# Segment mean over 10 million sorted ids: probe loads in eleven small groups between the data tiles, looks and gathers 18 rows ahead, no ring clear, branch at row 82

## The chip, the cores and the metric

The kernel runs on one core of a Trainium2 chip. The metric is the device time of one execution in microseconds (us), lower is better. "Span" is the profiled execution's own length; the time is 1.7 to 1.8 us longer. Runs were made on several chips. The changed kernel took the same time on two occasions, but the kernel before has slower states, told below, so each comparison says what it compares.

Names: VectorE (DVE), ScalarE (ACT), GpSimd (POOL), SyncE (SP, which here only issues loads).

## The reference

```python
def reference(data, segment_ids):          # 10,000,000 floats; sorted ids below 10,000
    num_segments = int(segment_ids.max()) + 1
    sums = np.zeros(num_segments, dtype=np.float32)
    counts = np.zeros(num_segments, dtype=np.float32)
    np.add.at(sums, segment_ids, data)
    np.add.at(counts, segment_ids, 1)
    return sums / np.maximum(counts, 1)
```

## The kernel before

Each of 128 partitions holds 78125 elements, cut into 98 "rows" of 800. A row has at most one boundary between two segments. To find it without reading all 80 MB of ids, the kernel

1. **probes**: loads every 160th id, 8 bytes at a time (5 columns a row, 489 in all), in row groups;
2. **looks** (`first_look`, VectorE, nine small operations): from a group's probes it finds which block of 160 holds the boundary, and writes an index;
3. **gathers** (GpSimd, one indirect DMA a row): fetches the 159 ids of that block into a ring of 36 row slots;
4. **looks a second time** (`second_look`, VectorE, six rows at once): sums the gathered ids, which gives the boundary `KK`;
5. **splits** (VectorE, one a row): sums the data left of the boundary; ScalarE sums the whole row (`total`).

At the end come carries, counts and two tables that are written out. A general path sits in a branch that is not taken with this input.

```python
GROUPS = [6, 8, 12, 12, 12, 12, 12, 12, 12]
RING = 36
...
    dpool = ctx.enter_context(tc.tile_pool(name="dpool", bufs=18))   # 18 data tiles of 2 rows
...
    GT = gpool.tile([P, RING, W], I64, name="GT")
    nc.gpsimd.memset(GT.bitcast(I32).rearrange("p a b -> p (a b)"), 0)
...
    def load_probes(g):
        a = 0 if g == 0 else K * bounds[g] + 1
        b = min(K * bounds[g + 1] + 1, NPR)
        nc.sync.dma_start(out=pr_flat[:, a:b], in_=ids_p[:, a * S : (b - 1) * S + 1 : S])
...
    def gather(g):
        for r in range(bounds[g], bounds[g + 1]):
            nc.gpsimd.indirect_dma_start(
                out=GT[:, r % RING, :], out_offset=None, in_=ids2d[:],
                in_offset=bass.IndirectOffsetOnAxis(ap=IDX[:, r : r + 1], axis=0),
                bounds_check=N - W, oob_is_err=False)

    def second_look(a, b):
        s = a % RING
        nc.vector.tensor_reduce(
            out=GS[:, a:b], in_=gt32[:, s : s + b - a, 0 : 2 * W : 2], axis=AX.X, op=ALU.add)
        kr = fpool.tile([P, b - a], FP32, name="kr")
        nc.vector.tensor_sub(out=kr, in0=QQ[:, a:b], in1=GS[:, a:b])
        nc.vector.tensor_mul(out=KK[:, a:b], in0=kr, in1=BT[:, a:b])

    def split(r):
        ...
        nc.vector.scalar_tensor_tensor(
            out=junk_v[:, 0:n], in0=iota[:, 0:n], scalar=KK[:, r : r + 1], in1=d,
            op0=ALU.is_lt, op1=ALU.mult, accum_out=A[:, r : r + 1])
...
    for r in range(-6, NR):
        while nt < NT and nt <= (r + 24) // 2:
            load_data(nt)
            nt += 1
            if pnext < NG:                       # one probe group after each early data tile
                load_probes(pnext)
                pnext += 1
        while lnext < NG and bounds[lnext] <= r + 30:
            first_look(lnext)
            lnext += 1
        while gnext < NG and bounds[gnext] <= r + 16:
            gather(gnext)
            gnext += 1
        ...
        if r >= done_k: second_look(done_k, min(done_k + 6, NR)); ...
        total(r); split(r)
        ...                                      # check at row 60, branch at 64, first table at 65
```

The program's order is not the order on an engine: the framework's scheduler emits each engine's instructions by its own estimate of when they will be ready, with program order as priority. Each engine then executes its list in that order.

## Time and profile before

| | before |
|---|---|
| time, fast runs | 231.4 us median (230.1 to 231.7) |
| span; VectorE busy | 230.0; 150.9 us |
| first gather starts, last ends | 19.7, 164.3 us |
| first split; splits left 4 us after the last gather | 62.3 us; 40 |
| last VectorE operation; tail after it | 217.4; 12.6 us |

The page first: 40 slices of 5.75 us, each digit the busy tenths of a slice; the last line is GB/s moved by the DMA.

```profile
span 230.0 us, 1186 instructions
...
DVE  4963102204298960351999999999299999999800
...
POOL 8914777777778777777878788788400000000110
DMA  6899999999999999999999999999749000000000
GB/s 81 102 142 144 231 160 204 239 131 230 237 124 375 409 397 397 398 403 402 399 400 402 399 403 401 401 399 412 303 170 369 14 0 0 0 0 0 2 5 0
```

The VectorE is idle for most of the first 60 us and solid, but for one slice, from about 109 us (slice 19, counted from 0) on. The DMA moves little in the first 70 us, while the 8-byte probes pass, then 400 GB/s.

The groups of the page (line, engine, operation, output<-input, count, then busy us and mean ns of one, then idle time before them and what ended most of it):

```profile
L324 POOL DMA_INDIRECT GT<-in_segment_ids_dram,IDX x98 | 115.0, 1174 | 36.8 <-issue 26.2
...
L295 DVE CAST q_114<-pr 128x13 f32<-128x13 int32 (+2 forms) x8 | 9.0, 1127 | 40.5 <-DMA pr<-in_segment_ids_dram 40.5
L335 DVE TENSOR_REDUCE GS<-GT 128x6 f32<-128x954 int32 (+1 forms) x17 | 18.7, 1099 | 23.1 <-DMA GT<-in_segment_ids_dram,IDX 21.5
...
L281 POOL MEMSET GT<- 128x11448 int32 x1 | 9.6, 9628 | 0.0
```

The clear (L281) takes 9.6 us. While it runs, the first cast of the VectorE does not end (start, length):

```profile
2.79 9.63 POOL L281 MEMSET GT<- 128x11448 int32 x1
```

```profile
4.83 7.62 DVE L295 CAST q_114<-pr 128x7 f32<-128x7 int32 x1 [2.39 <-DMA pr<-in_segment_ids_dram]
```

The waits (who waited for whom: total us, times, longest):

```profile
DVE q_114 L295 <- DMA pr<-in_segment_ids_dram: 40.5, 7, 8.3
...
DVE GS L335 <- DMA GT<-in_segment_ids_dram,IDX: 21.5, 4, 6.3
POOL GT L324 <- DVE IDX L315: 7.3, 1, 7.3
```

The VectorE waits mostly for probes.

The VectorE's timeline near the first split (start, length, ..., idle before it and releaser):

```profile
52.66 0.17 DVE L295 CAST q_114<-pr 128x13 f32<-128x13 int32 x1 [7.89 <-DMA pr<-in_segment_ids_dram]
...
53.76 0.17 DVE L315 SCALAR_TENSOR_TENSOR IDX<-NB,pos 128x12 int32<-128x12 f32 x1
54.06 1.15 DVE L335 TENSOR_REDUCE GS<-GT 128x6 f32<-128x954 int32 x1
61.59 0.17 DVE L295 CAST q_114<-pr 128x13 f32<-128x13 int32 x1 [6.38 <-DMA pr<-in_segment_ids_dram]
...
62.31 1.04 DVE L350 SCALAR_TENSOR_TENSOR junk_v<-iota,q_114,data_t 128x800 bf16<-128x800 f32 x1
```

The look of a later group (L295, index at L315) stands in front of the first second look (L335), and one more stands behind it, before the first split. The engine sits up to 8.3 us for a group's probes although the gathers of row 0 landed long before.

### The profile page before, as it was taken

Reading aid. Unit: us, or ns where it says so; the run is one execution under the profiler, and the core shown is the slowest. Engines: PE = TensorE matmul, PEld = TensorE weight load, DVE = VectorE, ACT = ScalarE, POOL = GpSimd, SP = SyncE. Lnnn points to the kernel's source line nnn. Section 1 sums busy time; section 2 is a strip of 40 time slices with the busy share of each in tenths; the row PEclk is TensorE's granted clock in tenths of the full one; section 3 lists DMA queues with packets and bytes.
Section 4 is the critical chain, followed back from the end, with each engine's and each line's share of the span. In section 5 each row is a group of like instructions: output and inputs, shape, how many; then the busy total and the mean of one; then the engine's idle time right before and its main releaser. Section 6 shows DMA issues by size and latency. Waiting matters only on the chain. (4 is left out here: it accounts for less than half of the span.)

```text
span 230.0 us, 1186 instructions
## 1 busy us (share of the span) xinstructions
PE 1.6 (1%) x6; PEld 1.4 (1%) x6; DVE 150.9 (66%) x432; ACT 95.4 (41%) x197; POOL 128.9 (56%) x114
## 2 busy tenths in 40 slices
PE   0000000000000100000000010000000000000000
PEld 0000000000000100000000000000000000000000
DVE  4963102204298960351999999999299999999800
ACT  2333023033032767676777787667746600000000
POOL 8914777777778777777878788788400000000110
DMA  6899999999999999999999999999749000000000
GB/s 81 102 142 144 231 160 204 239 131 230 237 124 375 409 397 397 398 403 402 399 400 402 399 403 401 401 399 412 303 170 369 14 0 0 0 0 0 2 5 0
DMA packets 74701, 53.39 MB, mean 232 GB/s; under 512 B 65274, under 2 KB 65357, under 8 KB 74688
## 3 DMA queue, kind: packets, MB, share of 16 engines
q1 hardware_dynamic: 69920, 40.51, 62.1%
q0 software_dynamic: 4768, 12.78, 19.2%
q14 instruction: 13, 0.11, 0.2%
HBM read 56.46 MB, written 0.04 MB: 246 GB/s over the span
## 5 line engine op out<-in xcount | busy, mean ns | idle before, releaser
L324 POOL DMA_INDIRECT GT<-in_segment_ids_dram,IDX x98 | 115.0, 1174 | 36.8 <-issue 26.2
L345 ACT ACTIVATE junk_a<-data_t 128x800 bf16<-128x800 f32 x98 | 85.0, 867 | 85.7 <-DMA data_t<-in_data_dram 81.7
L350 DVE SCALAR_TENSOR_TENSOR junk_v<-iota,q_114,data_t 128x800 bf16<-128x800 f32 x98 | 101.8, 1038 | 0.6
L295 DVE CAST q_114<-pr 128x13 f32<-128x13 int32 (+2 forms) x8 | 9.0, 1127 | 40.5 <-DMA pr<-in_segment_ids_dram 40.5
L335 DVE TENSOR_REDUCE GS<-GT 128x6 f32<-128x954 int32 (+1 forms) x17 | 18.7, 1099 | 23.1 <-DMA GT<-in_segment_ids_dram,IDX 21.5
L556 POOL DMA_INDIRECT out_dram<-out_139,AN x1 | 1.1, 1117 | 52.5 <-DVE FF L511 52.5
L345 ACT ACTIVATION_READ_ACCUMULATOR junk_a<-data_t 128x1 f32 x98 | 18.3, 186 | 0.0
L281 POOL MEMSET GT<- 128x11448 int32 x1 | 9.6, 9628 | 0.0
L298 DVE TENSOR_TENSOR eq<-pr 128x48 f32<-128x48 int32 (+2 forms) x9 | 9.2, 1025 | 0.0
L350 DVE DVE_READ_ACCUMULATOR junk_v<-iota,q_114,data_t 128x1 f32 x98 | 7.9, 81 | 0.0
L340 DVE TENSOR_TENSOR q_114<-kr,q_114 128x6 f32<-128x6 f32 (+1 forms) x17 | 2.7, 161 | 0.0
L339 DVE TENSOR_TENSOR kr<-QQ,GS 128x6 f32<-128x6 f32 (+1 forms) x17 | 2.7, 157 | 0.0
L301 DVE TENSOR_SCALAR ST<-jc 128x12 f32<-128x12 f32 (+2 forms) x9 | 2.1, 239 | 0.0
L556 POOL DMA_INDIRECT out_dram<-out_140,AN x1 | 1.0, 992 | 2.0 <-issue 2.0
L310 DVE TENSOR_SCALAR NB<-q_114 128x12 f32<-128x12 f32 (+2 forms) x9 | 1.8, 200 | 0.0
L300 DVE TENSOR_REDUCE jc<-eq 128x12 f32<-128x48 f32 (+2 forms) x9 | 1.7, 194 | 0.0
L345 ACT ACT_TABLE_LOAD x1 | 1.3, 1283 | 0.8 <-PEq L652 0.8
L314 DVE TENSOR_TENSOR pos<-ST,wb 128x12 f32<-128x12 f32 (+2 forms) x9 | 1.5, 164 | 0.1
L309 DVE TENSOR_TENSOR q_114<-q_114 128x12 f32<-128x12 f32 (+2 forms) x9 | 1.5, 166 | 0.1
L318 DVE SCALAR_TENSOR_TENSOR QQ<-q_114,ST 128x12 f32<-128x12 f32 (+2 forms) x9 | 1.5, 164 | 0.1
L315 DVE SCALAR_TENSOR_TENSOR IDX<-NB,pos 128x12 int32<-128x12 f32 (+2 forms) x9 | 1.5, 164 | 0.0
L527 DVE TENSOR_REDUCE out_139<-sel_133 128x48 f32<-128x624 f32 (+1 forms) x2 | 1.3, 628 | 0.0
(95 smaller groups left out, 29.5 us busy)
## 6 DMA issues: line engine op xcount, KB each, us to landing
data_t<-in_data_dram SPq DMA_DIRECT2D x48, 800.0 KB, 11.7
GT<-in_segment_ids_dram,IDX POOLq DMA_INDIRECT x98, 6.1
data_t<-in_data_dram SPq DMA_DIRECT2D x1, 662.5 KB
pr<-in_segment_ids_dram SPq DMA_DIRECT2D x6, 60.0 KB, 11.2
pr<-in_segment_ids_dram SPq DMA_DIRECT2D x1, 58.0 KB, 11.0
pr<-in_segment_ids_dram SPq DMA_DIRECT2D x1, 40.0 KB
pr<-in_segment_ids_dram SPq DMA_DIRECT2D x1, 31.0 KB, 4.0
snt<-in_segment_ids_dram SPq DMA_DIRECT2D x1, 1.0 KB
```

What stands on the lines that cost most here:

```text
L281: nc.gpsimd.memset(GT.bitcast(I32).rearrange("p a b -> p (a b)"), 0)
L295: nc.vector.tensor_copy(out=V[:, a : b + 1], in_=pr32[:, a : b + 1, 0])
L298: nc.vector.tensor_tensor(out=eq, in0=in0b, in1=in1b, op=ALU.is_equal)
L301: nc.vector.tensor_scalar(out=ST[:, a:b], in0=jc, scalar1=float(S), scalar2=float(1 + W), op0=ALU.mult, op1=ALU.add)
L310: nc.vector.tensor_scalar(out=NB[:, a:b], in0=BT[:, a:b], scalar1=-1.0, scalar2=1.0, op0=ALU.mult, op1=ALU.add)
L324: nc.gpsimd.indirect_dma_start(out=GT[:, r % RING, :], out_offset=None, in_=ids2d[:], in_offset=bass.IndirectOffsetOnAxis(ap=IDX[:, r : r ...
L335: nc.vector.tensor_reduce(out=GS[:, a:b], in_=gt32[:, s : s + b - a, 0 : 2 * W : 2], axis=AX.X, op=ALU.add)
L339: nc.vector.tensor_sub(out=kr, in0=QQ[:, a:b], in1=GS[:, a:b])
L340: nc.vector.tensor_mul(out=KK[:, a:b], in0=kr, in1=BT[:, a:b])
L345: nc.scalar.activation(out=junk_a[:, 0:n], in_=d, func=ACT.Copy, accum_out=T[:, r : r + 1])
L350: nc.vector.scalar_tensor_tensor(out=junk_v[:, 0:n], in0=iota[:, 0:n], scalar=KK[:, r : r + 1], in1=d, op0=ALU.is_lt, op1=ALU.mult, accum_ ...
L556: nc.gpsimd.indirect_dma_start(out=out2d[:], out_offset=bass.IndirectOffsetOnAxis(ap=AN[:, i : i + 1], axis=0), in_=o[:], in_offset=None,)
```

## The change

The intent: start splitting early. Probes come in smaller groups between the data tiles, 26 rows ahead, so that only 28 rows' worth stands before row 0 in program order. Looks and gathers come together, 18 rows ahead. The clear goes, as ids that are not gathered are multiplied by zero. The branch moves behind all loads and gathers.

```diff
-GROUPS = [6, 8, 12, 12, 12, 12, 12, 12, 12]
+GROUPS = [4, 6, 8, 10, 10, 10, 10, 10, 10, 10, 10]
+X_PROBE = 26
+X_LOOK = 18
...
-    nc.gpsimd.memset(GT.bitcast(I32).rearrange("p a b -> p (a b)"), 0)
...
-    IF_AT = 64
+    CHECK_AT = 78
+    IF_AT = 82
...
-    for r in range(-6, NR):
-        while nt < NT and nt <= (r + 24) // 2:
+    for r in range(-X_PROBE, NR):
+        while pnext < NG and bounds[pnext] <= r + X_PROBE:
+            load_probes(pnext)
+            pnext += 1
+            if pnext == 2:
+                nc.sync.dma_start(out=snt[0 : P - 1, :], in_=...)
+        while nt < NT and 2 * nt <= r + X_PROBE:
             load_data(nt)
             nt += 1
-            if pnext < NG:
-                load_probes(pnext)
-                pnext += 1
-        while lnext < NG and bounds[lnext] <= r + 30:
+        while lnext < NG and bounds[lnext] <= r + X_LOOK:
             first_look(lnext)
+            gather(lnext)
             lnext += 1
-        while gnext < NG and bounds[gnext] <= r + 16:
-            gather(gnext)
-            gnext += 1
...
-        if r == IF_AT - 4:
+        if r == CHECK_AT:
             keys(); check()
         if r == IF_AT:
-            counts(0, 60)
             with tc.If(...): general_path(...)
-        if r == C1 - 1:
-            counts(60, C1)
+            counts(0, C1)
             ...                                  # first table
```

More of the change, by code (lines that the diff above doesn't have):

```diff
@@ L565 @@
     NT = (NR + 1) // 2
-    load_probes(0)
     nc.vector.memset(snt32[:, 0:1], NSEG)
     nc.vector.memset(snt32[:, 1:2], 0)
-    nc.sync.dma_start(
-        out=snt[0 : P - 1, :],
-        in_=segment_ids[D : N].rearrange("(p d) -> p d", d=D)[:, 0:1],
-    )
-    load_data(0)
-    load_probes(1)
-    load_data(1)
-    load_probes(2)
-    nt = 2
-    IF_AT = 64
+    CHECK_AT = 78
+    IF_AT = 82
     C1 = 66
@@ L584 @@
     lnext = 0
-    pnext = 3
-    for r in range(-6, NR):
-        while nt < NT and nt <= (r + 24) // 2:
+    pnext = 0
+    nt = 0
+    for r in range(-X_PROBE, NR):
[3 more added lines that the diff above has]
+            if pnext == 2:
+                nc.sync.dma_start(
+                    out=snt[0 : P - 1, :],
+                    in_=segment_ids[D : N].rearrange("(p d) -> p d", d=D)[:, 0:1],
+                )
+        while nt < NT and 2 * nt <= r + X_PROBE:
             load_data(nt)
             nt += 1
-            if pnext < NG:
-                load_probes(pnext)
-                pnext += 1
-        while lnext < NG and bounds[lnext] <= r + 30:
+        while lnext < NG and bounds[lnext] <= r + X_LOOK:
             first_look(lnext)
+            gather(lnext)
             lnext += 1
-        while gnext < NG and bounds[gnext] <= r + 16:
-            gather(gnext)
-            gnext += 1
         if r < 0:
@@ L610 @@
             extend()
-        if r == IF_AT - 4:
+        if r == CHECK_AT:
+            assert lnext == NG
             keys()
@@ L614 @@
         if r == IF_AT:
-            counts(0, 60)
+            assert nt == NT
             with tc.If(nc.values_load(badi[0:1, 0:1], min_val=0, max_val=1) > 0):
```

## The prediction

> **What bounds the kernel now.** Span 230.0 us (the page), VectorE (DVE) busy 150.9 of it. The timeline has three stretches. (1) To about 62 us no row is split: the DVE waits 40.5 us for probes (the waits view). Probes are 8-byte reads, 489 columns x 128 = 62592 packets, all queued ahead of the first nine data tiles. In 10:70 us (the stretches view) the DMA moved about 11.0 MB, 27 us at the later 401 GB/s; the other 33 us went to 418 probe columns, 0.078 us a column, about 9.8 ns a packet on each of 16 engines. The Trainium skill (DMA: Bandwidth & Descriptors, Bandwidth) gives a floor of about 10.5 ns a packet; this agrees. (2) 62:102 us: only about 15 rows split; the DVE waits three times 5 to 6 us for gathers that GpSimd issues one per 1.3 us. (3) 102:217 us: DVE nearly solid, 83 rows at about 1.4 us (split 1.10, second look 1.25 per six rows, the rest looks, check, tables), less one 4.0 us hole at the branch. The DMA ends at 178 us, after a dry hole of 5 us: its queue engine lost 12 us at the branch. 12.6 us follow the last DVE operation. So the time is the late DVE start plus DVE work, not DMA.
>
> **What the change does.**
> - The 9.6 us GpSimd clear goes. It blocked the first DVE cast for 7.6 us; the Trainium skill (SBUF — State Buffer, Who interferes with whom) calls this an exclusive lock. With smaller first probe groups, the first gather should start near 6 to 8 us instead of 19.7.
> - Probes keep all their packets (38 us by the estimate), but only groups of rows 0 to 27 stand before row 0 in the DVE's order. First split near 20 to 28 us instead of 62.
> - Two more first looks: 2 to 3 us DVE. Gathers unchanged.
> - The branch at 82 comes after all loads and gathers are issued: no dry hole; a DVE hole of 2 to 4 us may stay.
>
> **New bound.** The DMA: 52.9 MB at 401 GB/s = 132 us, plus 38 us probes, plus 2 us start: about 172 us, 1.75 us a row, more than the DVE's 1.4. So the DVE becomes DMA-paced, with a lag: a look at group b waits for its probes, which land just before data row b, and rows b-18 and on may stand behind it in the DVE's order. The last probes (row 88) should land near 156 us. After that 18 to 28 rows are to be split at 1.3 us, with second looks, and up to 12 us of check, counts and tables: DVE ends near 190 to 206 us. Plus 12.6 us tail and 1.5 us from span to time: 204 to 220; if rows are scheduled closer to their data, 192 to 204.
>
> **Predicted: 206 us, 196 to 217.** Faster by over 2%: 0.90; within 2%: 0.06; slower: 0.04.
>
> **What would show it.** First gather before 9 us, first split before 30; no 7.6 us cast; DMA busy to about 172 us without a hole, at about 300 GB/s throughout; DVE gaps spread out, ended by probes and gathers; last DVE operation near 192; same packets and bytes.
>
> **What would make it wrong.** The instruction order on the DVE is the scheduler's, not the program's: a look placed too early makes the DVE wait in order, once per group, and could return the gain. The probes' time may hide behind other transfers, or grow when mixed. The branch at 82 may drain the pipeline. Buffers (18 tiles) could throttle loads if the DVE lags by over 36 rows.

## More of the kernel before

The 98 gathers keep GpSimd busy 115 us. With the 0.3 us between two of them (the 26.2 us "issue") they form a stream that is hardly ever kept waiting by an index.

GpSimd waits for an index once, at the start.

Counted in the emitted order, seven of the nine groups' indices are written before the first split, the other two after 3 and 23 splits. That makes the start late. It also means that GpSimd always has indices for many rows ahead.

## The result and the profile after

| | before | after |
|---|---|---|
| time, fast runs | 231.4 us (4 runs) | 254.2 us (253.9 to 254.4, 4 runs) |
| ratio | | 1.0995 (95%: 1.096 to 1.103) |
| first gather starts | 19.7 | 13.1 |
| first split | 62.3 | 27.7 |
| gaps of over 0.5 us in the gather stream | none | 9, 65.3 us in sum |
| last gather ends | 164.3 | 216.1 |
| splits left 4 us later | 40 | 13 |
| last VectorE operation | 217.4 | 239.8 |
| tail | 12.6 | 12.6 |

A ratio is the mean time of one kernel's fast runs over that of the other's of the same rounds, so not quite the ratio of the medians. A gap is the idle time on GpSimd between the end of one gather and the start of the next.

The sum closes. The last gather ends 51.8 us later: it starts 6.6 us earlier, has 65.3 us of gaps more, and the gathers with their small pauses take 6.9 us less (-6.6 + 65.3 - 6.9 = 51.8). After it 23.8 us pass until the VectorE is done, instead of 53.1: 29.4 us less. Together 22.4 us, which is the difference of the last VectorE operations.

The page, slices now of 6.3 us:

```profile
span 252.4 us, 1192 instructions
...
DVE  3220843861992495509708834975791991699900
...
POOL 3077157386047518710871574077377387100120
DMA  7999999999999999999999996783223223100000
GB/s 149 233 321 303 385 149 395 286 290 396 184 384 348 215 411 206 352 399 180 413 256 303 352 196 230 246 295 103 62 64 82 62 64 94 46 0 0 0 8 0
```

The VectorE starts early but is solid for no more than two slices on end until it has only 20 us of work left. GpSimd shows a hole every few slices. The DMA's load has fallen to a third or less for the last quarter of the span, so it is not what ends last.

The groups of the changed kernel's page that answer to those of before (L325 is the gather, L336 the second look, L296 the look's first cast):

```profile
L325 POOL DMA_INDIRECT GT<-in_segment_ids_dram,IDX x98 | 110.9, 1132 | 102.3 <-DVE IDX L316 29.0
...
L336 DVE TENSOR_REDUCE GS<-GT 128x6 f32<-128x954 int32 (+1 forms) x17 | 18.8, 1107 | 84.4 <-DMA GT<-in_segment_ids_dram,IDX 83.2
...
L296 DVE CAST q_114<-pr 128x11 f32<-128x11 int32 (+3 forms) x10 | 1.7, 168 | 7.8 <-DMA pr<-in_segment_ids_dram 7.8
```

And its waits, in the columns of before:

```profile
DVE GS L336 <- DMA GT<-in_segment_ids_dram,IDX: 83.2, 14, 11.9
...
POOL GT L325 <- DVE IDX L316: 29.0, 4, 10.5
...
POOL GT L325 <- DVE q_114 L341: 18.8, 2, 11.7
...
DVE q_114 L296 <- DMA pr<-in_segment_ids_dram: 7.8, 2, 6.2
```

The second looks now wait 83.2 us in all for gathers (21.5 before). The gathers' own idle time rose from 36.8 to 102.3 us, for operations of the VectorE: the index, or the operation next to it in the list. The waits for probes nearly vanished, from 40.5 to 7.8 us. So both engines wait, and for each other.

One round of it in the timeline, VectorE first:

```profile
113.52 1.15 DVE L336 TENSOR_REDUCE GS<-GT 128x6 f32<-128x954 int32 x1 [6.54 <-DMA GT<-in_segment_ids_dram,IDX]
114.58 0.16 DVE L296 CAST q_114<-pr 128x11 f32<-128x11 int32 x1
...
119.24 0.17 DVE L316 SCALAR_TENSOR_TENSOR IDX<-NB,pos 128x10 int32<-128x10 f32 x1
...
124.75 0.08 DVE L351 DVE_READ_ACCUMULATOR junk_v<-iota,q_114,data_t 128x1 f32 x1
133.73 1.15 DVE L336 TENSOR_REDUCE GS<-GT 128x6 f32<-128x954 int32 x1 [8.89 <-DMA GT<-in_segment_ids_dram,IDX]
```

and GpSimd over the same stretch:

```profile
106.97 1.00 POOL L325 DMA_INDIRECT GT<-in_segment_ids_dram,IDX  x1 [0.30 <-issue]
119.67 1.64 POOL L325 DMA_INDIRECT GT<-in_segment_ids_dram,IDX  x1 [11.70 <-DVE q_114 L341]
...
132.74 1.00 POOL L325 DMA_INDIRECT GT<-in_segment_ids_dram,IDX  x1 [0.30 <-issue]
```

Read the two together. At 113.52 the second look of rows 42 to 47 starts, after 6.54 us of waiting: those rows' gathers were issued last at 106.97, and GpSimd then had nothing to do. Only behind that wait stands the look for rows 48 to 57 (114.58). Its nine operations are spread between four splits, so its index is written at 119.24. GpSimd resumes at 119.67, after 11.70 us of idleness. It now issues ten gathers. On the VectorE five more splits stand before the next second look; it ends them at 124.8 and then waits 8.89 us for the sixth gather. Then the round begins anew, once per group.

Counted in the emitted order, the number of splits that stand before a group's index:

| first row of the group | 10 | 18 | 28 | 38 | 48 | 58 | 68 | 78 | 88 |
|---|---|---|---|---|---|---|---|---|---|
| after: splits before its index | 5 | 9 | 21 | 30 | 40 | 50 | 61 | 70 | 79 |

So an index is written 5 to 9 rows ahead of the group's first row, not 18. Raising `X_LOOK` from 18 to 26 makes the scheduler emit exactly the same order on VectorE, GpSimd, ScalarE and SyncE, so it was not run (this was seen by building both sources; it is no measurement): 18 is a priority, and it was not what held the looks back.

### The profile page after: what moved, and what is told of

It reads as the page before. It is cut to its first block, busy times and chain, and to the rows that moved or that the text cites. A ratio compares the mean times of both kernels' runs of the same rounds, so it can differ in the third digit from the quotient of the medians.

```text
span 252.4 us, 1192 instructions
## 1 busy us (share of the span) xinstructions
PE 1.6 (1%) x6; PEld 1.4 (1%) x6; DVE 144.3 (57%) x443; ACT 95.4 (38%) x197; POOL 115.2 (46%) x113
## 2 busy tenths in 40 slices
DMA packets 74733, 53.39 MB, mean 212 GB/s; under 512 B 65306, under 2 KB 65389, under 8 KB 74720
## 3 DMA queue, kind: packets, MB, share of 16 engines
q0 software_dynamic: 4768, 12.78, 18.3%
## 5 line engine op out<-in xcount | busy, mean ns | idle before, releaser
L325 POOL DMA_INDIRECT GT<-in_segment_ids_dram,IDX x98 | 110.9, 1132 | 102.3 <-DVE IDX L316 29.0
L336 DVE TENSOR_REDUCE GS<-GT 128x6 f32<-128x954 int32 (+1 forms) x17 | 18.8, 1107 | 84.4 <-DMA GT<-in_segment_ids_dram,IDX 83.2
L296 DVE CAST q_114<-pr 128x11 f32<-128x11 int32 (+3 forms) x10 | 1.7, 168 | 7.8 <-DMA pr<-in_segment_ids_dram 7.8
L299 DVE TENSOR_TENSOR eq<-pr 128x40 f32<-128x40 int32 (+3 forms) x11 | 2.1, 187 | 0.0
L301 DVE TENSOR_REDUCE jc<-eq 128x10 f32<-128x40 f32 (+3 forms) x11 | 2.0, 186 | 0.0
L302 DVE TENSOR_SCALAR ST<-jc 128x10 f32<-128x10 f32 (+3 forms) x11 | 1.8, 168 | 0.0
L310 DVE TENSOR_TENSOR q_114<-q_114 128x10 f32<-128x10 f32 (+3 forms) x11 | 1.8, 167 | 0.0
L319 DVE SCALAR_TENSOR_TENSOR QQ<-q_114,ST 128x10 f32<-128x10 f32 (+3 forms) x11 | 1.8, 162 | 0.0
L311 DVE TENSOR_SCALAR NB<-q_114 128x10 f32<-128x10 f32 (+3 forms) x11 | 1.8, 163 | 0.0
L315 DVE TENSOR_TENSOR pos<-ST,wb 128x10 f32<-128x10 f32 (+3 forms) x11 | 1.8, 162 | 0.0
L316 DVE SCALAR_TENSOR_TENSOR IDX<-NB,pos 128x10 int32<-128x10 f32 (+3 forms) x11 | 1.8, 161 | 0.0
## 6 DMA issues: line engine op xcount, KB each, us to landing
pr<-in_segment_ids_dram SPq DMA_DIRECT2D x7, 50.0 KB, 16.2
```

The lines of the kernel that those rows point to most:

```text
L299: nc.vector.tensor_tensor(out=eq, in0=in0b, in1=in1b, op=ALU.is_equal)
L301: nc.vector.tensor_reduce(out=jc, in_=eq, axis=AX.X, op=ALU.add)
L302: nc.vector.tensor_scalar(out=ST[:, a:b], in0=jc, scalar1=float(S), scalar2=float(1 + W), op0=ALU.mult, op1=ALU.add)
L310: nc.vector.tensor_sub(out=BT[:, a:b], in0=V[:, a + 1 : b + 1], in1=V[:, a:b])
L311: nc.vector.tensor_scalar(out=NB[:, a:b], in0=BT[:, a:b], scalar1=-1.0, scalar2=1.0, op0=ALU.mult, op1=ALU.add)
L325: nc.gpsimd.indirect_dma_start(out=GT[:, r % RING, :], out_offset=None, in_=ids2d[:], in_offset=bass.IndirectOffsetOnAxis(ap=IDX[:, r : r ...
```

## The experiments

**One part at a time.** Theory T1: the looks have too little lead, because their probes stand behind data tiles in the load queue. Rivals: R1, mixing 8-byte packets with the rest slows the transfers; R2, the late branch.

*e1: probes issued 44 rows ahead.*

```diff
-X_PROBE = 26
+X_PROBE = 44
+X_DATA = 26
...
-        while nt < NT and 2 * nt <= r + X_PROBE:
+        while nt < NT and 2 * nt <= r + X_DATA:
```

> The changed kernel with only the probe loads moved: issued 44 rows ahead of use instead of 26 (data tiles stay at 26, looks and gathers at 18). In the emitted VectorE order the looks of the ten-row groups then stand 14 to 22 rows ahead of their first row instead of 7 to 9. Theory T1 (too little lead: the look of a group stands in the VectorE order so close to the group's use that its gathers, 1.3 us each on GpSimd plus about 6 us landing, are waited for once a group): VectorE waits for gathers fall from 83 us to under 30, time about 200 to 212 us. Rival R1 (mixing 8-byte probes and gathers with data slows the transfers themselves): time stays within 2% of the changed kernel, 249 to 259 us. Rival R2 (the late branch and the tables behind it cost the time): stays at 245 to 255.

Measured: 241.2 us, correct. Looks did move (splits before the index of row 38: 17 instead of 30). But the waits of the second looks (L337 here) fell little:

```profile
DVE GS L337 <- DMA GT<-in_segment_ids_dram,IDX: 73.6, 12, 11.8
```

Gaps of the gather stream: 42.7 us. T1's number failed: leading looks alone recover little, because the scheduler now places the second looks earlier as well (rows 36 to 41 after 19 splits). The time lies below both rivals' ranges too, but on another chip than the changed kernel's, so it does not rule them out.

*e2: the clear put back into the changed kernel.*

> The changed kernel with only the GpSimd clear of the gather ring put back. On the chip the clear should cost up to 10 us at the start if only its busy time matters (rival: same or up to 4% slower than the changed kernel). But the emitted VectorE order moves with it: looks stand about 3 to 6 rows earlier (the look of rows 28 on after 15 splits instead of 21). T1 therefore expects it to be FASTER than the changed kernel: 25 to 50 us fewer gather waits, time 220 to 238 us.

Measured: 244.1 us (243.3 to 245.3), correct. Against 254.2 for the changed kernel (on other chips) it is faster, as T1 said and the rival did not, but by less than T1's range. Gaps 58.6 us, waits for gathers 62.9. So removing 9.6 us of work had cost time here. The emitted order moved with the clear (the index of row 28 after 15 splits instead of 21); that the order is how it cost time is argued, as clear and order changed together.

*e3: the kernel before, only the clear taken away.*

> The kernel before with only the clear taken away. Its emitted VectorE order changes too: only 4 groups of looks stand before the first split instead of 7, and the looks from row 38 on stand 25 to 48 rows ahead instead of 38 and more. T1 expects the lead to stay long enough, so the earlier start counts: first split about 40 us instead of 62, and time 205 to 222 us. Rival (the clear is what costs or protects by itself, order does not matter): 222 to 231, that is at most 8 us less than before.

Measured: 216.7 and 218.4 us in fast runs, 226.4 and 226.6 in slow ones, correct. Four looks, not seven, stand before the first split; first split at 36.5 us, no gap in the gather stream, last gather ends at 166.1 us. The longer lead is kept and the early start counts, as T1 expected.

*e4: the kernel before, check, branch and first table moved.*

> The kernel before with only the check at row 78, the branch at 82 and the first table behind it. R2 (the late branch costs): slower by 10 to 20 us. T1: within 2% of before, 227 to 236 us; the tables move behind the branch but the VectorE has the same work and stays busy from 100 us on; the 12 us hole of the load queue at the branch should disappear.

Measured: 250.4 us, correct. Neither theory may claim it. The order changed too: the second looks of rows 66 to 83 moved up to after 24 to 26 splits. Yet its waits for gathers were only 8.8 us in all (21.5 in the trace of before). What its trace shows instead is the stepping state described under e8, from 62 to 112 us: 11 splits start there, 19 in the trace of before. e14 and e15 test the branch properly.

On the chip of these four the kernel before took 239.8 to 241.9 us in the runs labelled fast, 4% more than on the others, where runs at 240 to 242 are labelled slow. The changed kernel was not run on it. The ratios (1.002 for e1, 1.015 for e2, 1.041 for e4) therefore say less than the traces.

**Hold the second looks back.** If second looks in front of looks are the trouble, a pin can test it. One column of an earlier split's result is copied into the second look's output before it, so the scheduler cannot place it earlier than that split:

```diff
     def second_look(a, b):
         s = a % RING
+        if a >= 4:
+            nc.vector.tensor_copy(out=GS[:, a : a + 1], in_=A[:, a - 4 : a - 3])
         nc.vector.tensor_reduce(out=GS[:, a:b], ...)
```

*e5: the changed kernel again.*

> The changed kernel again, unaltered, as the yardstick for the other three on this chip (the second chip ran the kernel before 4% slower than the first). Expected: 1.08 to 1.12 times the kernel before of the same rounds; nine gaps of over 0.5 us in the GpSimd gather stream, about 65 us in sum.

Measured: 254.2 us (252.1 to 254.4), nine gaps, 66.1 us. Only one run of the kernel before was fast in this job (232.6 us; the others 239.7 to 255.8), so 1.09 rests on one run.

*e6: the changed kernel with the pin at 4.*

> The changed kernel with one edit: each second look is pinned behind the split of the row 4 before its first (a one-column copy from that split's result into its output makes it wait), so that the scheduler cannot hoist second looks ahead of splits. Refined theory T1b: the loss is starvation of the GpSimd gather stream: looks stand in the VectorE's order behind second looks that wait for the previous gathers, so both engines wait in turn, and each look stands only 8 to 10 rows ahead of its use. The pin does not move the looks (still 8 to 10 rows ahead), so T1b expects little: gaps of the gather stream 50 to 75 us, time within 4% of the changed kernel (1.05 to 1.14 of before). Rival R4 (the hoisted second looks alone are the loss, the lead of the looks does not matter): 1.00 or below.

Measured: 221.9 us (221.4 to 222.2), correct. Gaps 33.9 us, and the waits view has for the second look

```profile
DVE GS L338 <- DMA GT<-in_segment_ids_dram,IDX: 41.3, 7, 11.2
```

against 83.2 us. My expectation was wrong: the time is 22 us below its range. The indices stand within two splits of where they stood (row 48 after 40 splits in both, row 88 after 78 instead of 79). What moved further are second looks: that of rows 42 to 47 from after 36 splits to after 41, so behind the next group's look. T1b's starvation is right, its stress on the lead is not: the relative order of the two kinds of look decides. R4 had forecast this result (0.95 of the one fast run of before). R1 falls with it, as the transfers are mixed as before.

*e7: e1 and e6 together.*

> Both edits: probes issued 44 rows ahead instead of 26, and second looks pinned. With the first alone (earlier run, 1.00 of before) looks stood 14 to 22 rows ahead, but second looks were hoisted behind them, still 74 us of waits. With both, 13 to 15 splits lie between a look and the second look that needs its gathers. T1b: gaps in the gather stream under 25 us, VectorE waits for gathers under 35 us, 0.88 to 0.94 of before. R4 and R1 (transfers slowed by the mixing): 0.98 or more.

Measured: 214.9 us (214.3 to 215.0), correct: 0.92 of the one fast run of before. Gaps 3.8 us. Its waits view for the look (L297) and the second look (L339):

```profile
DVE q L297 <- DMA pr<-in_segment_ids_dram: 30.1, 8, 6.0
...
DVE GS L339 <- DMA GT<-in_segment_ids_dram,IDX: 13.9, 3, 11.8
```

Waits for gathers are down to 13.9 us, of which 11.8 are the first second look's. The VectorE now waits for probes, that is for the load queue. This comes close to the DMA-paced kernel that the prediction described: the DMA moved 301 GB/s between 160 and 180 us and almost nothing after. R4 and R1 had 0.98 or more here; so the lead counts as well, once the second looks are held back.

*e8: the kernel before without the clear, with the pin at 4.*

> The kernel before without the clear (earlier run: about 0.90 of before, first split at 36 us, gather stream without gaps but 36 us of VectorE waits after the first split), with second looks pinned as well. T1b: same first split within 3 us, gather stream still without gaps, VectorE waits for gathers fall from 37 to under 20 us; 0.84 to 0.89 of before. If the pin does not help: 0.89 to 0.92.

Measured: 217.4 to 217.6 us in four fast runs, 0.935 of the one fast run of before, and no better than e3 (on another chip). Both ranges of the expectation failed. The profile fell in the one slow run (228.5 us span), so its waits are not compared with e3's. What it shows of the slow state, on the VectorE:

```profile
83.16 1.05 DVE L351 SCALAR_TENSOR_TENSOR junk_v<-iota,q,data_t 128x800 bf16<-128x800 f32 x1 [4.38 <-issue]
...
85.95 0.20 DVE L299 TENSOR_REDUCE jc<-eq 128x12 f32<-128x48 f32 x1 [1.66 <-remote]
88.75 1.05 DVE L351 SCALAR_TENSOR_TENSOR junk_v<-iota,q,data_t 128x800 bf16<-128x800 f32 x1 [2.60 <-remote]
```

From about 55 to 105 us the VectorE steps forward by a few operations and then stands, for up to 4.4 us. For the longer of these waits the profile names no operation of another engine of this core that ended them ("issue", "remote"), while GpSimd goes on issuing gathers, 1.3 to 2.0 us apart until 93 us. No fast run of e8 was profiled; in the fast profile of e3, splits of that stretch that wait for no gather follow at about 1.1 us.

**Dose and response.** T1c: what counts is that the look stands before the second look that waits for the previous group's last gathers. A recurrence by hand gives numbers: walk the emitted VectorE order with measured durations (split 1.05 us, second look 1.15); ten gathers follow an index at 1.31 us each; a gather lands about 5 us after its issue ends; transfers of data and probes are left out. It is an estimate from the traces. It was fitted to nothing, but e1, e2 and e5 to e8 had run when it was made; e9 and e10 had not. Recomputed from the order in the traces, every figure below came out within 1.3 us.

*e9: pin at 2.*

> The changed kernel with second looks pinned behind the split 2 rows before their first, instead of 4 (e6: 221.9 us, gaps of the gather stream 33.8 us). Theory T1c, revised after e6: what counts is what stands in the VectorE's order between the look of a group and the second look that waits for the previous group's last gathers; the look must come first. Hand recurrence from measured durations (gathers 1.31 us apart after their look, landing about 5 us after issue, splits 1.05, second look 1.15, VectorE in order, transfers left out), which gives gaps of 71 us for the changed kernel (measured 66) and 33 for e6 (measured 34), gives 15 us of gaps here: 12 to 22 us of gaps, waits for gathers 22 to 35 us, time 208 to 219 us, now near the limit of the transfers. Rival R5 (any pin helps equally, it only evens out the order): within 2% of e6, 217.5 to 226.

Measured: 219.3 us (ratio 0.946), correct. Gaps 29.8 us: outside my range, as was the time by 0.3 us. Waits for gathers 25.1 us, inside. The VectorE now waited 22.6 us for probes, which the recurrence leaves out; an index behind such a wait comes late.

*e10: pin at 6.*

> The same with the pin 6 rows before: the emitted order is nearly the changed kernel's own; looks in the same places within one split, second looks at most 5 splits later. T1c: recurrence gives 54 us of gaps (changed kernel 71, e6 33): 48 to 60 us of gaps, time 233 to 246 us. R5: 217 to 226.

Measured: 233.1 us in three fast runs (ratio 1.007; a slow one took 235.6), correct; gaps 51.9 us: both inside. Waits for gathers were 60.9 us. R5 is out. This is nearly the changed kernel's order, which makes one group a clean pair. The VectorE's timeline of e10 around the index for rows 48 on (L338 is the second look here):

```profile
102.93 0.08 DVE L353 DVE_READ_ACCUMULATOR junk_v<-iota,q,data_t 128x1 f32 x1
102.93 0.17 DVE L296 CAST q<-pr 128x11 f32<-128x11 int32 x1
...
107.58 0.08 DVE L353 DVE_READ_ACCUMULATOR junk_v<-iota,q,data_t 128x1 f32 x1
107.58 0.16 DVE L316 SCALAR_TENSOR_TENSOR IDX<-NB,pos 128x10 int32<-128x10 f32 x1
107.66 1.14 DVE L338 TENSOR_REDUCE GS<-GT 128x6 f32<-128x954 int32 x1
```

and GpSimd's:

```profile
100.53 1.08 POOL L325 DMA_INDIRECT GT<-in_segment_ids_dram,IDX  x1 [0.31 <-issue]
108.01 1.00 POOL L325 DMA_INDIRECT GT<-in_segment_ids_dram,IDX  x1 [6.41 <-DVE IDX L316]
```

The look still starts after 37 splits (36 in the changed kernel) and writes its index after 41 (40). But the second look of rows 42 to 47 (107.66) now stands behind it instead of in front, and the gap on GpSimd is 6.41 us instead of 11.70.

| | emitted order gives (gaps) | measured gaps | time |
|---|---|---|---|
| changed kernel | 71 | 65.3 | 254.2 |
| e2 clear | 68 | 58.7 | 244.1 |
| e10 pin 6 | 54 | 51.9 | 233.1 |
| e1 probes 44 | 42 | 42.7 | 241.2 |
| e6 pin 4 | 33 | 33.9 | 221.9 |
| e9 pin 2 | 15 | 29.8 | 219.3 |
| e7 probes 44, pin 4 | 0 | 3.8 | 214.9 |
| e13 probes 32, pin 3 | 0 | 16.2 | 217.6 |
| before | 0 | 0 | 231.4 |

Among the kernels with the same early probes (changed kernel, e10, e6, e9) the time falls with the gaps, though not in proportion (13.4 us of gaps and 21 us of time from the changed kernel to e10). The recurrence misses e9 and e13 by 15 and 16 us. Both wait over 20 us for probes, which it leaves out; but so does e7, which it misses by only 4. The kernel before has no gaps, but starts its splits at 62 us; e1's gaps are fewer than e10's, but it starts its splits 6 us later and ran on the chip where the kernel before was 4% slower.

*e11 and e12: looks 30 rows ahead, probes 44, pin 4; e12 with the branch at 64.*

> Probes 44 rows ahead, looks and gathers 30 ahead in the program (18 before), second looks pinned at 4, branch still at 82. T1c: no gap of the gather stream over 3 us in sum 6; the time is then set by the transfers (about 175 to 180 us to their end) and the VectorE work left after them: 205 to 216 us, no worse than e7 (214.9).

> e11 with the check back at row 60, the branch at 64 and the first table at row 65, as in the kernel before. Isolates the branch's place where no second look is hoisted: the loads still to be issued wait for the branch, so if the place matters through the load queue (the hole of 12 us seen in the kernel before) this is 3 to 10 us slower than e11; if the tables behind the late branch matter more, 2 to 6 us faster. T1c itself says nothing of it beyond: within 5% of e11.

Measured: 249.9 and 250.9 us, and WRONG results in both, by my mistake: a group of ten that starts 30 rows ahead reaches row r+39, and the ring has 36 slots. In program order rows 36 and 37 were gathered over rows 0 and 1 before these were read. The emitted code kept that order faithfully, so there is no race to find, and the first second look had to wait for the gathers of rows 36 and 37 (first split at 73.5 us). The two differ by 0.4% only.

**What was left.**

*e13: probes 32 ahead, pin 3.*

> The changed kernel with probes issued 32 rows ahead (26) and second looks pinned behind the split 3 rows before their first. Recurrence: no gaps of the gather stream, against 15 with the pin alone (e9, 219.3 us). In e7 (probes 44 ahead) the VectorE then waited 30 us for probes standing at the front of the load queue; with 32 these waits should be shorter. Expected 204 to 216 us, gaps under 8 us, waits for probes under 30 us.

Measured: 217.6 us (ratio 0.943), correct. Gaps 16.2 us, the time just above the range and 31.6 us of waits for probes: three misses. The intermediate lead did not remove the wait for probes.

*e14 and e15: a legal pair for the branch (looks 26 ahead, probes 36, pin 3): branch at 82, then at 66.*

```diff
-    CHECK_AT = 78
-    IF_AT = 82
+    CHECK_AT = 62
+    IF_AT = 66
```

> Probes 36 ahead, looks and gathers 26 ahead in the program (with groups of 10 that just fits the ring of 36, so results are right), second looks pinned at 3, branch at 82. Expected 204 to 218 us, gaps under 8 us; partner of the next run.

> The same with check at 62 and branch at 66 (in the emitted order after split 76 instead of 83). If the branch's place costs through the table behind it or through the drained loads, 3 to 10 us apart from e14; if it is small, as the pair e11 and e12 suggests (0.4% apart), within 1.5% of e14.

Measured: 217.8 and 221.6 us, both correct, ratios 0.943 and 0.959. In e14 the gaps were 11.9 us, over the 8 expected. The earlier branch is 3.8 us (1.7%) slower, so the place counts a little, but in the late branch's favour. That was measured in this pair's order of looks; there, the late branch is not what costs time.

*e16: e13 with the clear.*

> e13 with the GpSimd clear of the ring put back: the order of looks and second looks stays almost the same. The clear delays the first gathers little (they start at about 13 us without it, the clear ends at 12.4 us): expected 0 to 4 us slower than e13. If the clear really costs its 9.6 us on the chain: 8 to 11 us slower.

Measured: 221.4 us, correct, 3.8 us slower than e13 and within the expectation. But the order did not stay the same: the second looks stand where they stood, the looks of rows 18 on up to 6 splits earlier. The first gather starts 0.4 us later, the first split 2.8 us later, and waits for probes are 45.7 us instead of 31.6. So the pair does not isolate the clear; it shows that putting it back cost less than half of its 9.6 us here.

## Why the prediction was wrong

What held:

- **The early start.** First split at 27.7 us (predicted 20 to 28). The clear's removal freed the VectorE: before, the first cast of 7 columns took 7.6 us and ended with the clear; after, ten casts average 168 ns. The Trainium skill (SBUF — State Buffer, Who interferes with whom) describes that blocking as an exclusive lock, and both traces agree with it. The page has it for a VectorE operation in a two-port mode, casts among them; that this cast ran in one, no trace shows.
- **The small terms.** Same bytes (53.39 MB) and nearly the same packets (74701 and 74733); tail 12.6 us. The changed kernel doesn't contradict the estimate of 9.8 ns for an 8-byte packet on each of 16 engines: ScalarE, which follows the data tiles, summed its last row at 171.1 us, close to the 172 us predicted for the transfers.
- **The first gather** came at 13.1 us, not at 6 to 8. The first group's index waited in the VectorE's order behind the second group's probes (11.09 us). A small miss.

What failed is the step "**New bound. The DMA: ... So the DVE becomes DMA-paced**", and in it the line "Gathers unchanged". I costed gathers as work, 98 times 1.3 us, and saw that this was less than the DMA's 172 us. I did not cost them as a stream that has to be fed. In the kernel before nearly all indices exist before the first split, so the stream has no gap. In the changed kernel each index is written behind a second look that waits for the previous group's gathers, and each round costs the landing of the last gather (5.6 us after its issue ends), a second look (1.1 us), a look spread over four splits (4.7 us) and a start (0.4 us): 11.7 us in the round shown (the rounded terms add up to 11.8), 65.3 us over the nine gaps. That term, predicted as zero, is the error: DVE end 239.8 instead of 192. The chain of waits did not go through the load queue. VectorE waited 83.2 us for gathers and 7.8 us for probes; I had expected probes to matter.

Three runs show the cause. e10 against the changed kernel swaps a look and a second look, with the look in the same place, and takes 5.3 us off one gap. e6 moves second looks by up to 7 splits and looks by no more than two, and takes 32 us off the time. e7 removes the gaps and lands at 214.9 us, inside the predicted 196 to 217, with the waits for probes that I had described. That it lands there is partly luck: its probes are 44 rows ahead, and its VectorE ends at 199.9 us, not at 192. The prediction's text did name the scheduler's order as a danger, but the wrong way round (a look too early), and gave a slower result 4%.

What is settled and what isn't: the gaps and their cause are settled. The branch at 82 is not the cause, as far as e14 and e15 with their own order can tell. That the clear acts mainly through the emitted order (e2 and e3) is argued; no run changes the one without the other. Why the scheduler's estimate places a second look ahead of a look that would feed it was not examined; that it assumes gathers to be faster than they are is an inference. What causes the slow, stepping state is open, and so is e4.

The best version measured is e7 (changed kernel, probes 44 rows ahead, second looks pinned): 214.9 us against 231.4 and 254.2. Deleting the clear from the kernel before, one line, came within 4 us of it (e3, 216.7 and 218.4 us on another chip). e7's remaining 22 us between the last transfer and the last VectorE operation were not attacked.

## What to carry to other kernels

When two engines feed each other in rounds, cost the round trip, not only each engine's work: ask what stands in front of the operation that feeds the other engine, in the order in which the list is executed. After any structural edit, even the removal of a clear, read the emitted order first; a lead given in the source is only a priority. A dependency that holds a consumer back can be worth more than one that pulls a producer forward.

## What the Trainium skill lacked or had wrong

- DMA: Bandwidth & Descriptors (Anatomy of one DMA — SWDGE (gpsimd) path) fits a DMA of this queue as about 2.0 us plus bytes over 436 GB/s. For a gather of this kernel (12.78 MB over 98, so 130 KB) that gives an estimate of 2.3 us. The median from the start of the issue to landing was 6.1 us before and 5.7 us after. In the changed kernel's trace it depends on the loads: 6.1 us for the 49 gathers issued before 120 us, but 2.9 us, 1.0 of it the issue, for the 27 issued after 170 us, where the loads end. So the fit is not far off on a quiet queue; what the page lacks is a gather beside loads.
- The same page gives no issue rate for indirect DMAs. Here GpSimd issued one per 1.31 us in an undisturbed stretch (1.00 busy, 0.30 between), so 98 take 128 us even when nothing delays them.
- SBUF — State Buffer (Who interferes with whom) says that, against a VectorE operation in a two-port mode, whoever issues first gets the shared port and the other blocks. No page describes slower states of the same program: the kernel before ran at 230 to 233, 240 to 242 and 254 to 261 us. In a slow run of e8 the VectorE stood idle up to 4.4 us at a time, beside a gather stream without gaps until 93 us. That the shared port is behind it is not shown.
- Perfetto Trace Analysis (Identifying Dependency Chains) sends the reader to the semaphores. It lacks the case where the order of two operations on one engine makes the chain: 11.7 us of gap with one order, 6.4 us with the other.
